# Strided attention: key sums as four extra columns of the output matmuls, and keys transposed in 32x32 blocks on VectorE

## The chip, the cores and the metric

The kernel runs on 1 core of one Trainium2 chip. The metric is the device time of one execution in microseconds (us). A profile covers the "span", from the first traced instruction of the core to the last. The time is longer than the span by about 2 us. The record marks a state, fast or slow, for every run. All runs of this study are marked fast, so they can be compared; each kernel is compared with runs of the kernel before from the same rounds.

Engines go by the profile's names: PE (TensorE, matmuls), PEld (PE's weight loads), DVE (VectorE), ACT (ScalarE), POOL (GpSimd) and SP (SyncE, which issues all loads and stores here). PSUM is the memory that the matmuls of this kernel write to, and a bank is one part of it. A "traced row" is any record of an engine in the trace, its waits included.

## The reference

```python
def setup_inputs():
    batch, heads, seq, dim = (8, 12, 1024, 64)      # Q, K, V float32, stride 64
def reference(Q, K, V, stride):
    scale = 1.0 / np.sqrt(dim)
    for i in range(seq):
        attend_positions = np.arange(0, seq, stride)         # 16 keys of 1024
        scores = np.einsum('bhqd,bhkd->bhqk', q, k) * scale
        weights = np.exp(scores - max);  weights /= sum + 1e-10
        result[:, :, i, :] = np.einsum('bhqk,bhkd->bhqd', weights, v)
```

All of Q is read and the whole output is written (25 MB each), while only 16 keys and values of each head take part.

## The kernel before

A group `g` is four heads, and there are 24 groups. One load brings 1 MB of Q, one store takes 1 MB of output. In between: a cast to bf16 (GpSimd), a transpose in 32x32 blocks (VectorE), scores (PE), exp (ScalarE), outputs (PE), and the normalization. The parts that the change touches, with cuts marked `...`:

```python
def key_rows(m):                      # keys: scaled copies, one for each head of a group
    kr = k_raw[:, 4 * m : 4 * m + 4].rearrange("p n (q f) -> p n f q", f=2)
    for h in range(4):
        nc.scalar.activation(out=k_m[:, 4 * m : 4 * m + 4, :, h], in_=kr,
                             func=AF.Copy, scale=slot_m[:, h : h + 1])
def keys(m):                          # ... turned by PE, copied out by ScalarE
    for u in range(2):
        kp = psum_sc.tile(...)
        for i in range(2):
            for f in range(2):
                nc.tensor.matmul(kp[:, i, :, f], lhsT=k_m[...], rhs=perm_k..., start=True, stop=True)
        nc.scalar.copy(k_t[...], kp[...])
def sums_mm(g):                       # sums over the keys: four matmuls
    sm = sm_ps[g] = psum_s.tile([P, 8, 32], FP32, name="sm", tag="sm")
    for q in range(4):
        nc.tensor.matmul(sm[32 * q : 32 * q + 32], lhsT=sel32,
                         rhs=wt[g][:, :, 32 * q : 32 * q + 32],
                         start=True, stop=True, tile_position=(0, 32 * q))
def sums_rec(g):                      # ... turned, then one reciprocal of 32 elements
    nc.vector.transpose(smt..., sm_ps[g]...)
    nc.vector.reciprocal(rec[g], smt[:, :, 0:4])
def outputs(g, c):                    # c = 0, 1: four token blocks in two PSUM banks
    ...
    for i in range(4):
        nc.tensor.matmul(ps[:, i]..., lhsT=wt[g][:, 4 * c + i], rhs=vb[g]..., start=True, stop=True)
def normalize(g, c):                  # 6 of 8 blocks on VectorE, 2 by ScalarE copy and GpSimd multiply
    ...
# loop over g, shortened: without the tests for the last groups
    transpose(g + 2); scores(g + 1); outputs(g, 0); outputs(g, 1); sums_mm(g + 1)
    values(g + 2); cast(g + 3); normalize(g, 0); normalize(g, 1); sums_rec(g + 1)
    ...; store(g); load(g + QBUFS)    # QBUFS = 9 loads are issued ahead
```

The softmax here doesn't subtract the row's maximum and nothing guards it: scores larger than these inputs give would overflow.

## Time and profile before

| | before |
|---|---|
| time, median of 6 runs | 129.81 us (129.78 to 130.21) |
| span of the profiled run | 127.6 us |
| bytes moved | 51.12 MB, 401 GB/s over the span |
| transfer queue's share of the 16 engines | 96.6% |
| busiest engine | VectorE (DVE), 74% |
| last compute ends, last packet ends | 114.8 us, 125.8 us |

The lines that carry this are in the prediction. Beside them, these are the groups of instructions that the change removes or alters (page of the kernel before; line, engine, operation, out<-in, shapes, count | busy us, mean ns | idle before, releaser):

```profile
L278 DVE TENSOR_TENSOR out_sb<-o_ps,rec 128x1024 f32<-128x1024 f32 (+1 forms) x48 | 43.0, 932 | 0.5 <-PE o_ps L264 0.3
L282 POOL TENSOR_TENSOR out_sb<-out_sb,rec 128x512 f32<-128x512 f32 x24 | 25.0, 1042 | 5.3 <-ACT out_sb L277 5.3
L242 PE MATMUL sm<-w,sel 128*32 128x256 bf16 x96 | 12.7, 298 | 8.0 <-ACT w L233 5.9
L255 DVE RECIPROCAL rec<-smt 128x32 f32<-128x32 f32 x24 | 8.5, 353 | 2.7 <-POOL vb L203 0.5
L251 DVE STREAM_TRANSPOSE smt<-sm 128x256 f32<-128x256 f32 x24 | 10.3, 427 | 0.0
q14 instruction: 4, 0.03, 0.1%
```

A reciprocal of 32 elements costs 353 ns, half of what a multiply of 512 costs (675 ns; the 932 is the mean of this and of 1188 ns for 1024 elements). The last line counts the packets of one queue that bring instructions within the span; the experiments come back to it.

### The profile page before, as it was taken

To read this page: it belongs to the slowest core of one execution; us is meant where nothing else is said; L and a number is where in the kernel's file an instruction comes from. 1 tells how busy PE (TensorE), PEld (TensorE's weight loads), DVE (VectorE), ACT (ScalarE), POOL (GpSimd) and SP (SyncE) were. 2 spreads that over 40 slices of the span, in tenths; PEclk is the share of its full clock that TensorE was granted. 3 is DMA by queue.
4 is the path that set the end of the run, shared out by engine and by line. 5 is a ranking of instruction groups with operands and counts; after the bars stand their busy time and mean duration, and the time that the engine had idled before them with its cause. 6 is when DMAs were issued, how large, how long until landed. Compare 5 with 4: busy or idle time off the path is not lost. (4 is left out here: it accounts for less than half of the span.)

```text
span 127.6 us, 1413 instructions
## 1 busy us (share of the span) xinstructions
PE 74.9 (59%) x412; PEld 35.9 (28%) x412; DVE 94.8 (74%) x136; ACT 58.8 (46%) x91; POOL 90.5 (71%) x93
## 2 busy tenths in 40 slices
PE   0008399857777787778877396396395495920000
PEld 0003044333443433333333153142142241510000
DVE  6935639999998999999999669669678687890000
ACT  0453443996379775666555353443442541610000
POOL 8983499999969999996865965955956959150000
PEclk9999999999999999999999859959958965798555
DMA  2999989899899999899899899998998999999980
GB/s 61 373 315 483 452 370 483 349 398 475 372 431 444 393 444 467 367 472 447 362 480 431 372 490 406 398 501 347 444 470 352 452 403 429 424 426 426 429 370 39
DMA packets 7911, 51.20 MB, mean 401 GB/s; under 512 B 3872, under 2 KB 3872, under 8 KB 3872
## 3 DMA queue, kind: packets, MB, share of 16 engines
q1 hardware_dynamic: 7904, 51.12, 96.6%
q8 instruction: 3, 0.05, 0.2%
q14 instruction: 4, 0.03, 0.1%
HBM read 25.95 MB, written 25.17 MB: 401 GB/s over the span
## 5 line engine op out<-in xcount | busy, mean ns | idle before, releaser
L211 POOL CAST qb<-qn 128x2048 bf16<-128x2048 f32 x24 | 45.3, 1890 | 16.2 <-DVE out_sb L278 9.7
L233 ACT ACTIVATE w<-sc 64x512 bf16<-64x512 f32 x48 | 35.3, 736 | 44.5 <-PE sc L222 43.9
L278 DVE TENSOR_TENSOR out_sb<-o_ps,rec 128x1024 f32<-128x1024 f32 (+1 forms) x48 | 43.0, 932 | 0.5 <-PE o_ps L264 0.3
L222 PE MATMUL sc<-qt,k_t 128*128 128x512 bf16 x96 | 30.6, 447 | 18.2 <-DVE qt L215 17.2
L215 DVE STREAM_TRANSPOSE qt<-qb 128x1024 int32<-128x1024 int32 x24 | 29.2, 1215 | 15.3 <-POOL qb L211 15.3
L264 PE MATMUL o_ps<-vb,w 128*128 128x256 bf16 x192 | 31.6, 306 | 1.1 <-DVE out_sb L278 0.4
L282 POOL TENSOR_TENSOR out_sb<-out_sb,rec 128x512 f32<-128x512 f32 x24 | 25.0, 1042 | 5.3 <-ACT out_sb L277 5.3
L264 PEld LDWEIGHTS <-w 128*128 128x128 bf16 x192 | 19.8, 109 | 17.7 <-DVE out_sb L278 9.4
L222 PEld LDWEIGHTS <-k_t 128*128 128x128 bf16 x96 | 9.4, 103 | 30.8 <-issue 22.7
L242 PE MATMUL sm<-w,sel 128*32 128x256 bf16 x96 | 12.7, 298 | 8.0 <-ACT w L233 5.9
L203 POOL TENSOR_TENSOR vb<-mask,v_rep 128x256 bf16<-128x256 bf16 x24 | 16.0, 668 | 1.8 <-DVE v_rep L196 1.8
L277 ACT COPY out_sb<-o_ps 128x512 f32<-128x512 f32 x24 | 14.0, 585 | 2.9 <-POOL out_sb L282 1.5
L255 DVE RECIPROCAL rec<-smt 128x32 f32<-128x32 f32 x24 | 8.5, 353 | 2.7 <-POOL vb L203 0.5
L251 DVE STREAM_TRANSPOSE smt<-sm 128x256 f32<-128x256 f32 x24 | 10.3, 427 | 0.0
L242 PEld LDWEIGHTS <-sel 128*32 128x32 bf16 x96 | 4.7, 94 | 17.8 <-issue 14.9
L175 PE MATMUL kp<-perm_k,k_m 128*128 128x128 bf16 x24 | 2.3, 250 | 9.3 <-ACT k_m L165 9.3
L165 ACT ACTIVATE k_m<-k_raw,slot_m 128x256 bf16<-128x256 f32 x12 | 5.3, 518 | 1.2 <-DVE slot_m L153 1.2
L175 PEld LDWEIGHTS <-k_m 128*128 128x128 bf16 x24 | 1.7, 112 | 9.5 <-ACT k_m L165 9.3
L136 POOL MEMSET k_t<- 128x4608 bf16 x1 | 3.9, 3937 | 0.0
L183 ACT CAST k_t<-kp 128x512 bf16<-128x512 f32 x6 | 3.2, 589 | 0.9 <-PE kp L175 0.7
L165 ACT ACT_TABLE_LOAD x1 | 1.3, 1283 | 5.0 <-DMA k_raw<-in_K_dram 5.0
L146 DVE TENSOR_SCALAR s_sel<-col,slot_f 128x4 bf16<-128x4 int16 x1 | 3.1, 3142 | 0.1
(22 smaller groups left out, 10.8 us busy)
## 6 DMA issues: line engine op xcount, KB each, us to landing
qn<-in_Q_dram SPq DMA_DIRECT2D x24, 1024.0 KB, 17.6
out_dram<-out_sb SPq DMA_DIRECT2D x24, 1024.0 KB, 17.3
k_raw<-in_K_dram SPq DMA_DIRECT2D x1, 384.0 KB, 4.2
v_raw<-in_V_dram SPq DMA_DIRECT2D x1, 384.0 KB, 7.2
```

Source lines behind the costliest of these rows:

```text
L203: nc.gpsimd.tensor_tensor(out=vb[g], in0=mask, in1=v_rep[:, g // 2, g % 2].unsqueeze(1).to_broadcast([P, 4, D]), op=ALU.mult,)
L211: nc.gpsimd.tensor_copy(out=qb[g], in_=qn[g])
L215: nc.vector.transpose(qt[g].bitcast(I32), qb[g].bitcast(I32))
L222: nc.tensor.matmul(sc, lhsT=k_t[:, g, f, NK * (1 - e) : NK * (1 - e) + P], rhs=_ap_with(q, [q.ap[0], [D, 8], [16 * D, 2], [2, 32]], extra_ ...
L233: nc.scalar.activation(out=_ap_with(wa, [wa.ap[0], [P, 8], [1, 2], [2, 32]], extra_offset=64 * a), in_=sc[64 * a : 64 * a + 64].rearrange( ...
L242: nc.tensor.matmul(sm[32 * q : 32 * q + 32], lhsT=sel32, rhs=wt[g][:, :, 32 * q : 32 * q + 32], start=True, stop=True, tile_position=(0, 3 ...
L251: nc.vector.transpose(smt.rearrange("p i r -> p (i r)"), sm.rearrange("p i r -> p (i r)"))
L255: nc.vector.reciprocal(rec[g], smt[:, :, 0:4])
L264: nc.tensor.matmul(ps[:, i].rearrange("p s d -> p (s d)"), lhsT=wt[g][:, 4 * c + i], rhs=vb[g].rearrange("p s d -> p (s d)"), start=True, ...
L277: nc.scalar.copy(part(i0 + n, 4 - n), ps[:, n:4])
L278: nc.vector.tensor_tensor(out=part(i0, n), in0=ps[:, 0:n], in1=fact(i0, n), op=ALU.mult)
L282: nc.gpsimd.tensor_tensor(out=part(i0 + n, 4 - n), in0=part(i0 + n, 4 - n), in1=fact(i0 + n, 4 - n), op=ALU.mult,)
```

## The change

The intent: PE, ScalarE and VectorE spend instructions on sums and keys that can be had as a by-product. The values' operand gets four more columns that select the head, so an output matmul writes the four sums beside its 256 columns, in a PSUM bank of its own, already in the layout that the normalization needs. The keys are turned by VectorE's block transpose and small copies, without PE. The diff, cut to its core:

```diff
-    psum_o = ctx.enter_context(tc.tile_pool(name="po", bufs=2, space=bass.MemoryType.PSUM))
-    psum_s = ctx.enter_context(tc.tile_pool(name="psm", bufs=2, space=bass.MemoryType.PSUM))
+    psum_o = ctx.enter_context(tc.tile_pool(name="po", bufs=3, space=bass.MemoryType.PSUM))
...
+    v_bufs = []
+    for i in range(3):
+        v = const.tile([P, 4 * D + 4], BF16, name=f"v{i}")
+        nc.vector.tensor_copy(out=v[:, 4 * D :], in_=s_sel)
+        v_bufs.append(v)
...
     def key_rows(m):
-        (four scaled copies on ScalarE)
+        nc.scalar.copy(k_bf[:, part], k_raw[:, part])
+        nc.vector.transpose(k_r[:, part]... as int32, k_bf[:, part]... as int32)
-    def keys(m):
-        (8 matmuls, 2 copies)
+    def keys(m, c):
+        for s in range(4):
+            op = nc.vector.tensor_copy if m == 0 and s >= 2 else nc.scalar.copy
+            op(k_t[dst : dst + 32, ...], k_r[src : src + 32, ...])
...
-    def sums_mm(g): ...
-    def sums_rec(g): ...
     def outputs(g, c):                       # now c = 0 .. 3, two token blocks each
-        for i in range(4):
+        ps = psum_o.tile([P, 2, 512], FP32, name="o_ps", tag="o")
+        for i in range(2):
             nc.tensor.matmul(
+                ps[:, i, 0 : 4 * D + 4], lhsT=wt[g][:, 2 * c + i], rhs=vb[g],
                 start=True, stop=True)
-    def normalize(g, c): ...
+        ...                                  # r, o, to, by: views of the tiles
+        nc.vector.reciprocal(r, ps[:, :, 4 * D : 4 * D + 4])
+        if c < 3:
+            nc.vector.tensor_tensor(out=to, in0=o, in1=by, op=ALU.mult)
+        else:
+            nc.scalar.copy(to, o)
+            nc.gpsimd.tensor_tensor(out=to, in0=to, in1=by, op=ALU.mult)
...
```

More of the change, by code (lines that the diff above doesn't have):

```diff
@@ L80 @@
     qt_pool = ctx.enter_context(tc.tile_pool(name="qt", bufs=2))
-    vb_pool = ctx.enter_context(tc.tile_pool(name="vb", bufs=3))
     rec_pool = ctx.enter_context(tc.tile_pool(name="rec", bufs=2))
     psum_sc = ctx.enter_context(tc.tile_pool(name="psc", bufs=2, space=bass.MemoryType.PSUM))
-    psum_o = ctx.enter_context(tc.tile_pool(name="po", bufs=2, space=bass.MemoryType.PSUM))
-    psum_s = ctx.enter_context(tc.tile_pool(name="psm", bufs=2, space=bass.MemoryType.PSUM))
+    psum_o = ctx.enter_context(tc.tile_pool(name="po", bufs=3, space=bass.MemoryType.PSUM))
     ctx.enter_context(tc.manual_schedule())
@@ L109 @@
     id_v = identity.rearrange("p (c b a k) -> p c b a k", c=2, b=2, a=2)
-    perm_k = const.tile([P, 2, 2, 2, NK], BF16, name="perm_k")
     perm_v = const.tile([P, 2, 2, 2, 2, NK], BF16, name="perm_v")
@@ L118 @@
     nc.gpsimd.iota(col4, pattern=[[1, 4]], base=0, channel_multiplier=0)
-    for c in range(2):
-        for a in range(2):
-            nc.gpsimd.tensor_copy(out=perm_k[:, c, a], in_=id_v[:, c, :, a])
     for c in range(2):
@@ L148 @@
     )
-    sel32 = const.tile([P, 32], BF16, name="sel32")
-    nc.vector.memset(sel32, 0.0)
-    nc.vector.tensor_copy(out=sel32[:, 0:4], in_=s_sel)
-    slot_m = const.tile([P, 4], FP32, name="slot_m")
-    nc.vector.tensor_copy(out=slot_m, in_=s_sel)
+    v_bufs = []
[3 more added lines that the diff above has]
+        v_bufs.append(v)
     mask = const.tile([P, 4, D], BF16, name="mask")
     nc.vector.tensor_copy(out=mask, in_=s_sel.unsqueeze(2).to_broadcast([P, 4, D]))
-    k_m = const.tile([P, NC, 2, 4, 32], BF16, name="k_m")
+    k_bf = const.tile([P, NC, D], BF16, name="k_bf")
+    k_r = const.tile([P, NC, D], BF16, name="k_r")
     v_bf = const.tile([P, NC, D], BF16, name="v_bf")
@@ L162, in key_rows @@
     def key_rows(m):
-        kr = k_raw[:, 4 * m : 4 * m + 4].rearrange("p n (q f) -> p n f q", f=2)
-        for h in range(4):
-            nc.scalar.activation(
-                out=k_m[:, 4 * m : 4 * m + 4, :, h], in_=kr,
-                func=AF.Copy, scale=slot_m[:, h : h + 1],
-            )
-    def keys(m):
-        for u in range(2):
-            kp = psum_sc.tile([P, 2, 2, 2, 4 * NK], FP32, name="kp", tag="sc")
-            for i in range(2):
-                for f in range(2):
-                    nc.tensor.matmul(
-                        kp[:, i, :, f],
-                        lhsT=k_m[:, 4 * m + 2 * u + i, f].rearrange("p h q -> p (h q)"),
-                        rhs=perm_k.rearrange("p c a b k -> p c (a b k)"),
-                        start=True, stop=True,
-                    )
-            g0 = 8 * m + 4 * u
-            dst = k_t[:, g0 : g0 + 4]
-            nc.scalar.copy(
-                _ap_with(dst, [dst.ap[0], [KW, 8], [32, 4], [1, NK]], extra_offset=NK),
-                kp.rearrange("p i c f (s k) -> p (i c f) s k", s=4),
+        part = slice(4 * m, 4 * m + 4)
+        nc.scalar.copy(k_bf[:, part], k_raw[:, part])
+        nc.vector.transpose(
+            k_r[:, part].rearrange("p n d -> p (n d)").bitcast(I32),
+            k_bf[:, part].rearrange("p n d -> p (n d)").bitcast(I32),
+        )
+    def keys(m, c):
+        for s in range(4):
+            src, dst, col = 32 * (2 * c + s % 2), 32 * (2 * (s % 2) + s // 2), NK + 32 * s
+            op = nc.vector.tensor_copy if m == 0 and s >= 2 else nc.scalar.copy
+            op(
+                k_t[dst : dst + 32, 8 * m + c : 8 * m + 8 : 2, :, col : col + NK],
+                k_r[src : src + 32, 4 * m : 4 * m + 4].rearrange(
+                    "p n (a k f) -> p a n f k", a=2, f=2
+                )[:, s // 2],
             )
@@ L190, in value_rows @@
         for c in range(2):
-            vp = psum_s.tile([P, NC // 2, D], FP32, name="vp", tag="sm")
+            vp = psum_sc.tile([P, NC // 2, D], FP32, name="vp", tag="sc")
             nc.tensor.matmul(
@@ L196, in value_rows @@
             nc.vector.tensor_copy(out=v_rep[:, 6 * n : 6 * n + 6, c], in_=vp)
-    qb, qt, wt, vb, rec, out_sb, o_ps, sm_ps = {}, {}, {}, {}, {}, {}, {}, {}
+    qb, qt, wt, vb, rec, out_sb = {}, {}, {}, {}, {}, {}
     def values(g):
-        vb[g] = vb_pool.tile([P, 4, D], BF16, name="vb", tag="vb")
+        vb[g] = v_bufs[g % 3]
         nc.gpsimd.tensor_tensor(
-            out=vb[g], in0=mask,
+            out=vb[g][:, 0 : 4 * D].rearrange("p (s d) -> p s d", s=4), in0=mask,
             in1=v_rep[:, g // 2, g % 2].unsqueeze(1).to_broadcast([P, 4, D]),
@@ L237, in scores @@
             )
-    def sums_mm(g):
-        sm = sm_ps[g] = psum_s.tile([P, 8, 32], FP32, name="sm", tag="sm")
-        for q in range(4):
-            nc.tensor.matmul(
-                sm[32 * q : 32 * q + 32], lhsT=sel32,
-                rhs=wt[g][:, :, 32 * q : 32 * q + 32],
-                start=True, stop=True, tile_position=(0, 32 * q),
-            )
-    def sums_rec(g):
-        sm = sm_ps[g]
-        smt = rec_pool.tile([P, 8, 32], FP32, name="smt", tag="smt")
-        nc.vector.transpose(
-            smt.rearrange("p i r -> p (i r)"), sm.rearrange("p i r -> p (i r)")
-        )
-        rec[g] = rec_pool.tile([P, 8, 4], FP32, name="rec", tag="rec")
-        nc.vector.reciprocal(rec[g], smt[:, :, 0:4])
     def outputs(g, c):
@@ L260, in outputs @@
             out_sb[g] = out_pool.tile([P, 4, 8, D], FP32, name="out_sb", tag="out_sb")
-        ps = psum_o.tile([P, 4, 4, D], FP32, name="o_ps", tag="o")
-        o_ps[g, c] = ps
-        for i in range(4):
+            rec[g] = rec_pool.tile([P, 8, 4], FP32, name="rec", tag="rec")
+        ps = psum_o.tile([P, 2, 512], FP32, name="o_ps", tag="o")
+        for i in range(2):
             nc.tensor.matmul(
-                ps[:, i].rearrange("p s d -> p (s d)"), lhsT=wt[g][:, 4 * c + i],
-                rhs=vb[g].rearrange("p s d -> p (s d)"),
+                ps[:, i, 0 : 4 * D + 4], lhsT=wt[g][:, 2 * c + i], rhs=vb[g],
                 start=True, stop=True,
             )
-    def normalize(g, c):
-        ps = o_ps[g, c]
-        i0 = 4 * c
-        n = 4 if c == 0 else 2
-        part = lambda k, m: out_sb[g][:, :, k : k + m].rearrange("p s i d -> p i s d")
-        fact = lambda k, m: rec[g][:, k : k + m].unsqueeze(3).to_broadcast([P, m, 4, D])
-        if n < 4:
-            nc.scalar.copy(part(i0 + n, 4 - n), ps[:, n:4])
-        nc.vector.tensor_tensor(
-            out=part(i0, n), in0=ps[:, 0:n], in1=fact(i0, n), op=ALU.mult
-        )
-        if n < 4:
-            nc.gpsimd.tensor_tensor(
-                out=part(i0 + n, 4 - n), in0=part(i0 + n, 4 - n),
-                in1=fact(i0 + n, 4 - n), op=ALU.mult,
-            )
+        r = rec[g][:, 2 * c : 2 * c + 2]
+        o = ps[:, :, 0 : 4 * D].rearrange("p i (s d) -> p i s d", s=4)
+        to = out_sb[g][:, :, 2 * c : 2 * c + 2].rearrange("p s i d -> p i s d")
+        by = r.unsqueeze(3).to_broadcast([P, 2, 4, D])
+        nc.vector.reciprocal(r, ps[:, :, 4 * D : 4 * D + 4])
[4 more added lines that the diff above has]
+            nc.gpsimd.tensor_tensor(out=to, in0=to, in1=by, op=ALU.mult)
     def store(g):
@@ L297 @@
     cast(1)
+    keys(0, 0)
     transpose(0)
-    keys(0)
+    scores(0)
+    keys(0, 1)
     nc.vector.tensor_copy(out=v_bf, in_=v_raw)
-    scores(0)
     transpose(1)
@@ L306 @@
     cast(2)
-    sums_mm(0)
-    sums_rec(0)
     for g in range(NG):
@@ L313 @@
             scores(g + 1)
-        outputs(g, 0)
-        outputs(g, 1)
-        if g + 1 < NG:
-            sums_mm(g + 1)
         if g + 2 < NG:
@@ L321 @@
             cast(g + 3)
-        normalize(g, 0)
-        normalize(g, 1)
-        if g + 1 < NG:
-            sums_rec(g + 1)
+        for c in range(4):
+            outputs(g, c)
         if g in (1, 5):
             key_rows(g // 4 + 1)
-        if g in (2, 6):
-            keys(g // 4 + 1)
-        if g == 3:
+        if g in (2, 3, 6, 7):
+            keys(g // 4 + 1, g % 4 - 2)
+        if g == 4:
             value_rows(1)
```

## The prediction

> **What bounds the kernel now.** I read the busy table and the slices first, then the transfer rows, then SyncE's timeline, then VectorE's, and last the stretches of the tail.
>
> ```profile
> PE 74.9 (59%) x412; PEld 35.9 (28%) x412; DVE 94.8 (74%) x136; ACT 58.8 (46%) x91; POOL 90.5 (71%) x93
> DMA  2999989899899999899899899998998999999980
> q1 hardware_dynamic: 7904, 51.12, 96.6%
> ```
>
> No engine is above 74%, while the transfer engines are at 8 or 9 tenths in every slice but the first and the last, and the one transfer queue fills 96.6% of their time. The program must move 51.12 MB. I counted the packet records of the trace: from 9 us on, between 15.2 and 16.3 of the 16 engines carry a packet in every microsecond until 123.7 us, so there is no hole a change of compute could close.
>
> ```profile
> 105.00:110.00 5.00, 3.43 (x16) 1.50 (x15) 3.66 (x5) 1.36 (x4) 3.55 (x4) 0.50 1.02 429
> 110.00:115.00 5.00, 2.24 (x16) 1.11 (x14) 4.45 (x6) 1.88 (x3) 2.08 (x2) 0.99 1.01 423
> 115.00:120.00 5.00, 0.00 (x0) 0.00 (x0) 0.00 (x0) 0.00 (x0) 0.00 (x0) 0.69 1.02 428
> 120.00:125.00 5.00, 0.00 (x0) 0.00 (x0) 0.00 (x0) 0.00 (x0) 0.00 (x0) 0.50 0.85 357
> ```
>
> These are stretches (columns: PE, PEld, DVE, ACT, POOL busy, granted clock, transfer share, GB/s). All compute ends before 115 us; transfers go on at 423 to 428 GB/s for 9 us more. That is a backlog of stores already issued. The chain that ended last is therefore a queue of bytes, and the compute before it has about 9 us to spare less one transfer.
>
> ```profile
> 67.30 0.59 SPq L35 DMA_DIRECT2D out_dram<-out_sb  x1
> 69.64 0.47 SPq L35 DMA_DIRECT2D qn<-in_Q_dram  x1
> 72.19 0.59 SPq L35 DMA_DIRECT2D out_dram<-out_sb  x1
> ```
>
> On SyncE, one store follows the other after 4.89 us here. A group of four heads is one load and one store of 1.05 MB, and 2.10 MB at 428 GB/s is 4.90 us: the loop runs at transfer speed. What the engines could do is seen where neither loads nor buffers hold them up:
>
> ```profile
> 44.99 0.35 DVE L255 RECIPROCAL rec<-smt 128x32 f32<-128x32 f32 x1
> 45.26 1.19 DVE L215 STREAM_TRANSPOSE qt<-qb 128x1024 int32<-128x1024 int32 x1
> 46.37 1.78 DVE L278 TENSOR_TENSOR out_sb<-o_ps,rec 128x1024 f32<-128x1024 f32 x2
> 48.07 0.42 DVE L251 STREAM_TRANSPOSE smt<-sm 128x256 f32<-128x256 f32 x1
> 48.60 0.35 DVE L255 RECIPROCAL rec<-smt 128x32 f32<-128x32 f32 x1
> ```
>
> VectorE goes round in 48.60 - 44.99 = 3.61 us without a gap. So it has 4.90 - 3.61 = 1.29 us of slack per group, and this slack is what the change spends.
>
> **What the Trainium skill says.** "DMA: Bandwidth & Descriptors", section "Where 436 GB/s comes from", puts the fabric's ceiling at 435 GB/s, and says that about 358 GB/s of HBM per core binds a transfer between HBM and SBUF. The trace agrees with the first (423 to 434 GB/s held for tens of microseconds) and not with the second; the measurement decides: this kernel runs at the ceiling. "VectorE: DVE Perf Modes", section "First, the fixed hardware budget", says that a reciprocal is an iterative divide with a repeat count of 8. The trace fits a dear reciprocal: 32 elements take 353 ns, while an f32 multiply of 512 takes 675. "Perfetto Trace Analysis", section "Optimizing Scalar/DVE Operations", warns of a cost per instruction, larger from PSUM, part of which overlaps the next instruction. The trace shows the overlap: a multiply that starts at 39.85 and lasts 0.67 is followed at 40.45 us, a step of 0.60.
>
> **The change part by part**, per group unless said.
>
> *PE.* Removed: four key-sum matmuls with their weight loads (96 of 298 ns and of 94 ns, 17.4 us busy in all). Added: four columns on each of eight output matmuls, 256 to 260, at some 306 x 4/256 = 5 ns each, nothing. At the start and twice later, 24 key matmuls go. PE is not the bound: 0 us.
>
> *VectorE.* Removed: the transpose of the sums (427 ns) and one reciprocal of 32 elements. The normalizing multiplies were one of 1024 and one of 512 elements, and become three of 512. Added: four reciprocals of 8 elements out of PSUM. Their duration: transposes of 1024 and 256 elements take 1215 and 427 ns, so 1.03 ns an element and 164 ns fixed. With the same fixed part the reciprocal costs (353 - 164)/32 = 5.9 ns an element, and one of 8 costs 164 + 47 = 0.21 us (an estimate; the most it could be is 0.35, all fixed). Each multiply must wait for its own reciprocal, and such a dependent pair shows a gap of 0.11 us (48.07 + 0.42 to 48.60). So the steps are: transpose of the queries 1.11 (45.26 to 46.37); three times 0.21 + 0.10 + 0.60 = 0.91, so 2.73; the fourth reciprocal 0.21 less the overlap of 0.08, so 0.13. Sum 3.97 us against 3.61: 0.36 us longer, still under 4.90.
>
> *GpSimd.* Unchanged: 1890 + 1042 + 668 ns = 3.60 us. But its multiply now waits for the fourth reciprocal, the last thing that VectorE does for a group. From there multiply, values and cast take 3.6 us before the transpose that needs them, one whole round (3.97) later. It fits, by 0.3 us.
>
> *ScalarE.* The same copy of 512 elements; key rows and key copies only at the start and in six iterations.
>
> *PSUM.* Three output buffers of two banks for four blocks a group. The fourth block waits until the first is read; it then has two blocks of VectorE work (1.8 us) to get two matmuls (0.6 us) and the copy (585 ns) done. No wait on VectorE.
>
> *Start.* Keys are ready earlier without four scaled copies, eight matmuls and two copies out, but the scores start at 10.91 us because the first transpose ends at 10.77, behind the cast that waited for its load until 7.60. This stays. The second load is what the next cast waits for (11.76). So the keys gain nothing. The first store comes later: VectorE's first multiply begins at 19.79 now; then 2.73 + 0.21 puts the last reciprocal at 22.7, GpSimd's 1.04 makes 23.8, and the store is issued at about 23.9 instead of 22.09. In the packet records the initial loads last until 28.0 us, and from issue to the first packet the key load shows 1.1 us (0.73 to 1.83). So 23.9 is 3 us early enough: no hole.
>
> *End.* The 24th store is issued at the latest at 23.9 + 23 x 3.97 = 115.2, plus about 2 us for what is done once (two value copies of 524 ns, two small key transposes, and perhaps 0.4 us where the value matmuls now borrow the score buffers): 117. It was 114.9. The transfers end at 123.8 if never starved; the last store needs 2.45 us of them and 1.1 us ahead of them, so any issue before 120.2 costs nothing. 3 us remain. On the path to the end, the sum is 0.
>
> **The rivals.**
> 1. *VectorE becomes the bound.* For: the slack counted to the end is thin; each 0.01 us on a reciprocal is 0.04 a group and 0.9 us at the end, so 0.25 instead of 0.21 eats the 3 us. A PSUM source and two separated runs of four might be dearer than my fixed part. Against: multiplies from PSUM show the same fixed part (675 and 1188 ns for 512 and 1024: 162 ns). At 0.28 the last store would be at 123.4 and the time 133; at 0.35, 24 rounds of 4.53 give about 139.
> 2. *A chain of hand-overs becomes the bound*: multiply on GpSimd behind the fourth reciprocal, then the cast, then the transpose; or PE, which can now run less far ahead. With 0.3 us of margin in the first a round of 4.2 to 4.3 is possible: the last store at 122 to 124, time 131.5 to 134.
> 3. *The start gets faster and all follows.* For: PE and ScalarE are relieved there. Against: the transfers are busy from 3 us on with loads that wait for no compute; earlier keys can't start a byte earlier. At most 0.3 us.
> 4. *The transfer pattern shifts.* Stores are later against loads, so the small dips (15.2 to 15.6 engines at 34, 61 and 97 us) move. Worth 0.1 to 0.3 us either way.
>
> **Range and chances.** The base is 129.81 unchanged, plus 0.1 for rivals 1 and 2 weighed: 129.9. Below, nothing but rival 4: 129.4. Above, a VectorE round of about 4.15 us instead of 3.97 (last store 121.2) gives 131 and a little more: 131.6. Faster by 2% would need 2.6 us of fewer bytes or fuller engines: 0.01. Slower by 2% needs a round of about 4.25 us or more: 0.09. The rest is 0.90.
>
> **What would show it.** Right: the queue's share stays near 96.6%, the transfers end near 124 us of the span, the unhindered VectorE round is 3.9 to 4.1 us, four reciprocals of about 0.2 us, first store near 24 us, last store issued before 120. Wrong: a transfer share that sinks in the last 30 us, VectorE without idle time to the end, or reciprocals over 0.25 us. GpSimd waiting for VectorE's reciprocals and transposes waiting for the cast in turn would show rival 2.

## The result, and the profile after

| | before | after |
|---|---|---|
| time, median of 6 runs | 129.81 us | 129.36 us (129.15 to 129.72) |
| ratio, 95% interval | | 0.9959, 0.9941 to 0.9977 |
| span of the profiled run | 127.6 us | 127.9 us |
| time less span, same run | 2.14 us | 1.79 us |
| first store issued | 22.1 us | 24.6 us |
| last store issued | 114.9 us | 118.3 us |
| last packet ends | 125.8 us | 126.2 us |

A ratio is the mean time of one kernel's fast runs over that of the other's of the same rounds, so it is not quite the ratio of the medians quoted beside it.

The change is within 2%, as predicted, but 0.04 us below the range, whose lower end was 129.4. And the profile has no gain to show: this profiled run's span is 0.3 us longer than that of the kernel before. The page of the kernel after, in the parts shown before:

```profile
PE 65.9 (52%) x292; PEld 28.2 (22%) x292; DVE 100.3 (78%) x215; ACT 55.9 (44%) x96; POOL 90.2 (71%) x89
DMA  2999989999899899999899899899999999999970
q1 hardware_dynamic: 7904, 51.12, 96.4%
q14 instruction: 5, 0.04, 0.1%
L244 DVE TENSOR_TENSOR out_sb<-o_ps,rec 128x512 f32<-128x512 f32 x72 | 49.8, 692 | 2.5
L247 POOL TENSOR_TENSOR out_sb<-out_sb,rec 128x512 f32<-128x512 f32 x24 | 25.0, 1042 | 22.0 <-ACT out_sb L246 22.0
L246 ACT COPY out_sb<-o_ps 128x512 f32<-128x512 f32 x24 | 14.1, 586 | 45.3 <-DVE rec L242 16.8
L242 DVE RECIPROCAL rec<-o_ps 128x8 f32<-128x8 f32 x96 | 18.3, 192 | 0.8 <-PE o_ps L234 0.8
```

PE lost 9 us of work and VectorE gained 5.5. The transfers' row is as full as before (96.4 against 96.6%). The reciprocals of 8 elements take 192 ns (estimate: 210). GpSimd's wait for ScalarE's copy has grown from 5.3 to 22.0 us, and the copy now waits for the reciprocal. The stretches of the tail (PE, PEld, DVE, ACT, POOL busy, clock, transfer share, GB/s):

```profile
105.00:110.00 5.00, 2.92 (x16) 1.40 (x17) 4.86 (x11) 1.97 (x4) 3.89 (x4) 1.00 1.02 428
110.00:115.00 5.00, 3.24 (x19) 1.29 (x17) 4.80 (x15) 2.53 (x4) 1.58 (x2) 0.98 1.01 424
115.00:120.00 5.00, 0.23 (x2) 0.00 (x0) 1.42 (x4) 0.59 (x1) 1.55 (x2) 0.50 1.01 424
120.00:125.00 5.00, 0.00 (x0) 0.00 (x0) 0.00 (x0) 0.00 (x0) 0.00 (x0) 0.50 0.82 346
```

Compute now runs into the stretch from 115 us on, where it had ended before, yet the transfers flow at the same 424 to 428 GB/s. SyncE's timeline shows that the loop is no longer paced by transfers (after; start us, us, instruction):

```profile
76.65 0.59 SPq L35 DMA_DIRECT2D out_dram<-out_sb  x1
...
80.37 0.59 SPq L35 DMA_DIRECT2D out_dram<-out_sb  x1
...
84.78 0.59 SPq L35 DMA_DIRECT2D out_dram<-out_sb  x1
...
88.51 30.29 SPq L35 DMA_DIRECT2D out_dram<-out_sb  x9
```

Stores follow each other by 3.72 and 4.41 us in turn, 4.07 on average, where they had been 4.9 apart. That is not a speed-up: before, compute ran ahead until it had to wait for loads; now it is slower and never catches up with them, and the backlog of transfers is what hides this. The last line is nine stores merged: the last was issued at 88.51 + 30.29 less its own 0.5, so at 118.3 us. What sets these rounds, the timeline of all engines shows (after, from 54 us; the bracket is the idle time before and its releaser):

```profile
54.00 0.20 DVE L242 RECIPROCAL rec<-o_ps 128x8 f32<-128x8 f32 x1
54.23 0.59 ACT L246 COPY out_sb<-o_ps 128x512 f32<-128x512 f32 x1 [0.49 <-DVE rec L242]
...
54.71 1.25 DVE L203 STREAM_TRANSPOSE qt<-qb 128x1024 int32<-128x1024 int32 x1 [0.51 <-POOL qb L199]
...
54.90 1.04 POOL L247 TENSOR_TENSOR out_sb<-out_sb,rec 128x512 f32<-128x512 f32 x1 [0.22 <-ACT out_sb L246]
...
55.90 0.67 POOL L191 TENSOR_TENSOR v<-mask,v_rep 128x256 bf16<-128x256 bf16 x1
...
56.51 1.89 POOL L199 CAST qb<-qn 128x2048 bf16<-128x2048 f32 x1
...
58.37 0.20 DVE L242 RECIPROCAL rec<-o_ps 128x8 f32<-128x8 f32 x1
58.48 1.19 DVE L203 STREAM_TRANSPOSE qt<-qb 128x1024 int32<-128x1024 int32 x1
```

The copy of the fourth block does not need the reciprocal's result, yet it starts 0.03 us after the reciprocal ends (0.03 to 0.08 us in all 24 groups). Both read the same PSUM tile. The Trainium skill, "PSUM — Partial Sum Buffer", section "PSUM bank collisions raise a hardware error", says that two engines must not touch the same bank at once, reads against reads included, so such reads have to be put in order. The trace agrees in so far as the copy never overlaps the reciprocal; no run here shows a collision. So reciprocal, copy, multiply, values, cast and the next transpose are one chain of 4.28 us from 54.20 to 58.48, longer than VectorE's own round of 3.72. The rounds alternate because the chain makes VectorE wait only every second time: when it waits the 0.51 us before 54.71, its fourth reciprocal is already done (54.00), so the next chain gets a head start and its transpose comes 3.77 us after this one; in the round after that VectorE waits again (4.36 us).

So there are two questions. Where do 0.45 us come from, when nothing in the span got faster? And is the slower round really free?

### The profile page after: what moved, and what is told of

It reads as the page before. It is cut to its first block, busy times and chain, and to the rows that moved or that the text cites. A ratio compares the mean times of both kernels' runs of the same rounds, so it can differ in the third digit from the quotient of the medians.

```text
span 127.9 us, 1221 instructions
## 1 busy us (share of the span) xinstructions
PE 65.9 (52%) x292; PEld 28.2 (22%) x292; DVE 100.3 (78%) x215; ACT 55.9 (44%) x96; POOL 90.2 (71%) x89
## 3 DMA queue, kind: packets, MB, share of 16 engines
q1 hardware_dynamic: 7904, 51.12, 96.4%
## 4 chain that ended last, share of the span: by engine, by line
POOL 46%; issue 25%; DMA 16%; SPq 1%; DVE 1%; POOLq 1%; ACT 0%
POOL qb L199 27%; POOL v L191 10%; DMA out_dram<-out_sb 9%; POOL out_sb L247 9%; DMA qn<-in_Q_dram 7%; DVE qt L203 1%; POOLq L318 1%; SPq L35 1%; ACT out_sb L246 0%; SPq L100 0%; DVE v_rep L184 0%; SPq L98 0%; POOLq L199 0%; POOLq L247 0%; POOLq L191 0%
## 5 line engine op out<-in xcount | busy, mean ns | idle before, releaser
L234 PE MATMUL o_ps<-v,w 128*128 128x260 bf16 x192 | 40.6, 314 | 34.9 <-DVE out_sb L244 28.0
L244 DVE TENSOR_TENSOR out_sb<-o_ps,rec 128x512 f32<-128x512 f32 x72 | 49.8, 692 | 2.5
L234 PEld LDWEIGHTS <-w 128*128 128x128 bf16 x192 | 17.4, 108 | 61.4 <-DVE out_sb L244 40.7
L242 DVE RECIPROCAL rec<-o_ps 128x8 f32<-128x8 f32 x96 | 18.3, 192 | 0.8 <-PE o_ps L234 0.8
L191 POOL TENSOR_TENSOR v<-mask,v_rep 128x256 bf16<-128x256 bf16 x24 | 16.0, 668 | 2.3 <-DVE v_rep L184 2.3
L210 PEld LDWEIGHTS <-k_t 128*128 128x128 bf16 x96 | 10.4, 108 | 24.6 <-issue 16.6
L169 ACT COPY k_t<-k_r 32x128 bf16<-32x128 bf16 x20 | 5.9, 295 | 2.4 <-DVE k_r L159 2.1
L180 PE MATMUL vp<-v_bf,perm_v 128*128 128x384 bf16 x4 | 1.6, 412 | 2.7 <-DVE v_rep L184 2.4
L169 DVE COPY k_t<-k_r 32x128 bf16<-32x128 bf16 x4 | 2.5, 628 | 0.1
L184 DVE CAST v_rep<-vp 128x384 bf16<-128x384 f32 x4 | 2.0, 532 | 0.6 <-PE vp L180 0.6
L158 ACT CAST k_bf<-k_raw 128x256 bf16<-128x256 f32 x3 | 1.2, 405 | 2.9 <-DMA k_raw<-in_K_dram 2.8
```

The costliest lines, as they stand in the source:

```text
L169: op(k_t[dst : dst + 32, 8 * m + c : 8 * m + 8 : 2, :, col : col + NK], k_r[src : src + 32, 4 * m : 4 * m + 4].rearrange("p n (a k f) -> p ...
L191: nc.gpsimd.tensor_tensor(out=vb[g][:, 0 : 4 * D].rearrange("p (s d) -> p s d", s=4), in0=mask, in1=v_rep[:, g // 2, g % 2].unsqueeze(1).t ...
L210: nc.tensor.matmul(sc, lhsT=k_t[:, g, f, NK * (1 - e) : NK * (1 - e) + P], rhs=_ap_with(q, [q.ap[0], [D, 8], [16 * D, 2], [2, 32]], extra_ ...
L234: nc.tensor.matmul(ps[:, i, 0 : 4 * D + 4], lhsT=wt[g][:, 2 * c + i], rhs=vb[g], start=True, stop=True,)
L242: nc.vector.reciprocal(r, ps[:, :, 4 * D : 4 * D + 4])
L244: nc.vector.tensor_tensor(out=to, in0=o, in1=by, op=ALU.mult)
```

## The experiments

Eleven runs were made, all of the changed kernel or the one before, unchanged (e1, e11) or with a small edit, and all correct except one. The summary; "outside" is time less span, from each run's own pair (spans to 0.1 us, so a single value is good to 0.05; the six runs of the kernel before in the first comparison have no spans and count in the medians alone):

| kernel | runs | median us | ratio (95%) | mean span | outside, mean (range) |
|---|---|---|---|---|---|
| before, as the comparison | 33 | 129.80 to 129.95 by batch | 1 | 127.75 | 2.15 (2.09 to 2.21) |
| after, first comparison | 6 | 129.36 | 0.9959 (0.9941 to 0.9977) | 127.58 | 1.79 (1.75 to 1.82) |
| e1 before again | 5 | 129.84 | 1.0001 (0.9988 to 1.0014) | 127.74 | 2.15 (2.11 to 2.21) |
| e2 keys only | 5 | 129.58 | 0.9973 (0.9961 to 0.9985) | 127.78 | 1.78 (1.74 to 1.82) |
| e3 sums only | 6 | 129.54 | 0.9971 (0.9958 to 0.9985) | 127.73 | 1.80 (1.77 to 1.83) |
| e4 after, PE padded | 5 | 129.51 | 0.9972 (0.9960 to 0.9984) | 127.76 | 1.79 (1.76 to 1.82) |
| e5 before, VectorE + 8 | 4 | 129.41 | 0.9958 (0.9943 to 0.9972) | 127.65 | 1.77 (1.73 to 1.80) |
| e6 before, GpSimd + 8 | 4 | 129.93 | 1.0001 (0.9988 to 1.0014) | 127.78 | 2.15 (2.12 to 2.18) |
| e7 after, split block first | 6 | 129.69 | 0.9982 (0.9966 to 0.9998) | 127.88 | 1.79 (1.73 to 1.83) |
| e8 after, VectorE delayed | 4 | 133.31 | 1.0247 (1.0221 to 1.0274) | 131.43 | 1.80 (1.74 to 1.82) |
| e9 transfers alone | 4 | 127.96 | 0.9843 (0.9815 to 0.9870) | 126.17 | 1.80 (1.75 to 1.83) |
| e10 before, VectorE + 2 | 6 | 129.73 | 0.9990 (0.9974 to 1.0005) | 127.80 | 1.93 (1.90 to 1.95) |
| e11 after again | 6 | 129.47 | 0.9968 (0.9943 to 0.9993) | 127.72 | 1.80 (1.77 to 1.84) |

### e1: the kernel before again

The edit: none.

> The kernel before, unchanged, to learn its span in several runs (only one is known: 127.6 us of a time of 129.77, so 2.14 us lie outside the traced span; the changed kernel has 1.75 to 1.82 us outside in six runs and spans of 127.4 to 127.9). Theory A, the gain of 0.45 us lies outside the span: time less span stays near 2.1 us in all its runs, spans 127.5 to 127.9, about those of the changed kernel. Theory B, the transfers inside the span are packed better by the change: its spans are about 0.4 us longer than those of the changed kernel and time less span is about 1.8 in most runs. Ratio to the kernel before: 1.000 for both.

Measured: 2.11 to 2.21 us outside in these five runs and in the eleven of the comparison, with spans of 127.6 to 128.0. Theory A, a gain outside the span, holds; theory B, better packed transfers, finds no support.

### e2: only the keys

```diff
 (the kernel before, with the change's key_rows, keys and their calls)
-    perm_k, slot_m, k_m and the 24 key matmuls
+    k_bf, k_r: nc.scalar.copy, nc.vector.transpose, small copies
```

> Only the keys' half of the change: keys by 32x32 blocks on VectorE, the sums as before. Theory A (outside the span, by the length of the programs): PE loses only 24 of its 412 matmuls, so most of the gap of 0.35 us outside stays: 129.7 to 129.8. Theory C, that ready keys start the work earlier: the gain of 0.45 is here, 129.3 to 129.4. Theory B (stores come later against loads because VectorE's round is longer): 129.8, as the round stays at 3.6 us.

Measured: 129.58, ratio 0.9973. This fits none of the three: more gain than theory A allowed if PE's length were the cause, less than theory C promised. What does hold is the place: 1.78 us outside, and spans (127.6 to 127.9) like those of the kernel before.

### e3: only the sums

```diff
 (the changed kernel, with perm_k, slot_m, k_m, key_rows and keys of the kernel before)
-    k_bf, k_r and the copies
+    the 24 key matmuls and their copies
```

> Only the sums' half: four extra columns, the keys by PE as before. Theory A: PE loses 96 matmuls with their weight loads, so most of the gain shows, outside the span: 129.4 to 129.5, time less span 1.8. Theory B: the gain shows too, 129.4, but in the span. Theory C: 129.8.

Measured: 129.54, ratio 0.9971, 1.80 outside. Each half alone brings the full 0.36 us outside the span, and both together bring no more. So it is a step and not a sum of savings. Removed work that adds up would not do that.

### e4: PE's count restored

```diff
         for i in range(2):
+            for _ in range(PAD[2 * c + i]):          # (1, 0, 1, 0, 1, 1, 1, 0)
+                nc.tensor.matmul(ps[:, i, 4 * D : 4 * D + 4], lhsT=wt[g][:, 2 * c + i],
+                                 rhs=vb[g][:, 4 * D : 4 * D + 4], start=True, stop=True)
             nc.tensor.matmul(ps[:, i, 0 : 4 * D + 4], ...)
```

> The changed kernel with 120 added matmuls of four columns that write what the real ones overwrite, so that PE has as many matmuls and weight loads as before (412). [...] Theory A, if it is PE's instruction count that sets the time outside: back to 129.75 to 129.85 with 2.1 us outside. Theory B and C: stays at 129.4 with 1.8 us outside.

Measured: 129.51 with 1.79 outside. (The added matmuls took 182 ns each, 21.3 us in all, and the mean span, 127.76, did not grow.) PE's count is not the cause, and theory A in the form I had given it fell. The trace's packet records gave the next form. Apart from the loads and stores they hold a few packets of 8 KB on one instruction queue (q14), and their last one differs:

| profiled run | last instruction packet, us from the span's start | span ends | time |
|---|---|---|---|
| before | 129.23 to 129.73 | 127.63 | 129.77 |
| e1, before again | 129.23 to 129.68 | 127.62 | 129.77 |
| after | 127.89 to 128.20 | 127.93 | 129.72 |
| e2 | 127.30 to 127.66 | 127.59 | 129.37 |
| e3 | 127.75 to 128.10 | 128.00 | 129.78 |
| e4 | 127.47 to 127.94 | 127.69 | 129.47 |

(If the time is counted from the span's start, the two columns compare directly.) All have a packet close to the span's end, but only the kernel before has one more, 1.6 us behind it, and its time ends within 0.1 us of that packet. Whose program is it? In e2 a packet came at 116.7 us, when VectorE had run 192 of its 195 traced rows. The kernel before has 189, so the same place in the program would lie just behind its end. The traces of the changed kernel and its variants (after, e3, e4, and later e7, e8 and e11), with 235 to 265 rows, have such a packet too, far from the end, at 96.2 to 104.1 us, and there VectorE has run 193 to 197 rows each time.

### e5 and e6: eight more instructions on VectorE, or on GpSimd

```diff
     nc.gpsimd.memset(k_t[:, 8:NG], 0.0)
+    spare = const.tile([P, 8], FP32, name="spare")
+    for i in range(8):
+        nc.vector.memset(spare[:, i : i + 1], 0.0)      # e6: nc.gpsimd.memset
```

> The kernel before with eight one-element memsets added on VectorE at the start, where it idles. All 17 runs of the kernel before had 2.11 to 2.21 us outside the span and all 27 runs of the four other kernels 1.74 to 1.83, with the same spans; so the gain lies outside. Padding PE back to its old count did not bring it back, so it is not PE's count. The traces show one 8 KB packet of instructions at 129.23 us, 1.6 us behind the end of the span, only in the kernel before. Theory A2: it belongs to VectorE, whose program is 189 traced rows long in the kernel before, while in the keys-only kernel (195 rows) such a packet comes at row 192, inside the span. Eight more instructions pull it into the span: time less span 1.8, time 129.4 to 129.6, ratio about 0.997. Theory A3 (another engine's program, or the epilogue for another reason): 2.15 us outside, 129.85.

> The control: the same eight memsets on GpSimd instead. Theory A2 (VectorE's program): nothing changes, 2.15 us outside and 129.85. Theory A3 with GpSimd as the engine: 1.8 outside, 129.5.

(The first text counts 27 runs of the four other kernels; it should be 22.) Measured: e5 129.41, ratio 0.9958, 1.77 outside; e6 129.93, ratio 1.0001, 2.15 outside. Eight useless instructions on VectorE make the kernel before as fast as the changed one, and the same eight on GpSimd do nothing. The pages show the packet move: this is the instruction queue's row, first of e5, then of e6.

```profile
q14 instruction: 5, 0.04, 0.1%
```

```profile
q14 instruction: 4, 0.03, 0.1%
```

Five packets within the span, as in the kernel after, against four, as in the kernel before. In e5 the additional one came at 117.0 us, while VectorE sat at row 194 of 197 and waited for the stores. In e6 it came at 129.40, ending at 129.95 with the time at 129.94.

### e10: two more instructions

The edit, against e5:

```diff
-    for i in range(8):
+    for i in range(2):
         nc.vector.memset(spare[:, i : i + 1], 0.0)
```

> The kernel before with two instead of eight memsets added on VectorE. Eight pulled the packet of instructions into the span (at row 194 of 197) and took 0.37 us off the time outside. With two the program is 191 traced rows long, so a boundary near row 194 still lies behind the end. If it is the place of that boundary, nothing is gained: 2.15 us outside and 129.9. If any change of VectorE's program or of the layout does it: 1.8 and 129.5.

Measured: 129.73, 1.93 us outside (1.90 to 1.95 in six runs). Neither: the packet still lies behind the span, as I had expected, but it starts at 128.67 instead of 129.23 and ends 0.3 us before the time does. So there is no all or nothing, and my sentence that nothing is gained while the packet lies behind the end was wrong. A reading that fits: the nearer the boundary lies to the end of the program, the earlier the packet is asked for, and the less of it is in the way. But here the time goes on for 0.3 us after the packet, so the time outside is not simply set by the packet's end.

### e11: the changed kernel again

The edit: none.

> The changed kernel again, on another chip and in other rounds. Its first six runs had spans of 127.4 to 127.9 us, 0.1 to 0.2 below the mean of the kernel before, beside 0.36 us less outside the span. If the part in the span is scatter, the ratio here is 0.9965 to 0.998 (0.36 us of 129.9 is 0.9972) and the spans have the mean of the kernel before, 127.7 to 127.8; if the changed kernel's transfers really are better packed, the ratio is again 0.996 or less and the spans average 127.6 or less.

Measured: ratio 0.9968, mean span 127.72, 1.80 outside. So the 0.53 us of the first ratio (0.9959) were 0.36 outside and 0.17 in the span, and the second part did not repeat. Over both batches the changed kernel's twelve spans average 127.65 against 127.75 in 33 of the kernel before, less than their own scatter (127.4 to 128.3) lets one call a difference.

### e7: the split block first

```diff
-        if c < 3:
+        if c > 0:
             nc.vector.tensor_tensor(out=to, in0=o, in1=by, op=ALU.mult)
         else:
             nc.scalar.copy(to, o)
```

> The changed kernel, but with block 0 of a group instead of block 3 going over ScalarE's copy and GpSimd's multiply. In the changed kernel the copy starts only after the fourth reciprocal (20 to 30 ns after it ends), so copy, multiply, values, cast and the next transpose form one chain, and VectorE's rounds alternate between 3.72 and 4.41 us. If that chain is what makes the mean round 4.07 instead of 3.72, the rounds are 3.72 here wherever the loads don't hold, and the last store is issued at 112 to 116 instead of 118.3 us. If transfers bound the end (my prediction), the time stays all the same at 129.2 to 129.6 with 1.8 us outside. If the hand-over chain did reach the end, the time falls by 1 us or more.

Measured: 129.69, spans 127.5 to 128.3, 1.79 outside. The chain is indeed gone. VectorE's transposes and SyncE's last stores (e7, timelines):

```profile
47.26 1.24 DVE L203 STREAM_TRANSPOSE qt<-qb 128x1024 int32<-128x1024 int32 x1
...
50.98 1.23 DVE L203 STREAM_TRANSPOSE qt<-qb 128x1024 int32<-128x1024 int32 x1
...
54.70 1.24 DVE L203 STREAM_TRANSPOSE qt<-qb 128x1024 int32<-128x1024 int32 x1
```

```profile
71.84 0.59 SPq L35 DMA_DIRECT2D out_dram<-out_sb  x1
...
76.96 0.59 SPq L35 DMA_DIRECT2D out_dram<-out_sb  x1
...
81.86 0.59 SPq L35 DMA_DIRECT2D out_dram<-out_sb  x1
```

VectorE's rounds are 3.72 us from 47 us on. The stores follow each other by some 4.9 us from 67 us on, and VectorE's rounds from 81 us on, as in the kernel before. The last store is issued at 116.6 us instead of 118.3, a little later than the 112 to 116 that I had expected. The time does not follow (129.69 against 129.36 and 129.47 of the changed kernel, in other batches; it is 0.09 above the range that I gave for no effect, but the intervals of the ratios overlap): a chain of 0.35 us a round that I had overlooked costs nothing at the end.

### e8: VectorE delayed

```diff
         for c in range(4):
             outputs(g, c)
+        nc.vector.memset(spare, 0.0)          # 576 elements, 0.54 us
```

> The changed kernel with one more VectorE memset of about 0.6 us per group. The last store was issued at 118.3 us, and by my prediction an issue up to 120.2 costs nothing. If the round grows by 0.25 to 0.6 us, the last store is issued at 124 to 132 us, and the time is 129.4 plus (issue - 120.2), so 133 to 141 us. If the end had more slack than I worked out, the time grows by clearly less than issue - 120.2; if transfers were not the bound at all, by the whole shift of the issue from 118.3.

Measured: 133.31 (ratio 1.0247). VectorE's rounds are 4.32 us, and the last store was issued at 126.1 us in the profiled run, which took 133.52. By my formula it should have been 129.4 + 126.1 - 120.2 = 135.3; had transfers not been the bound, the shift of the issue from 118.3 would have made 137.2. So a transfer-bound end with more slack than I had worked out. The stretches (e8) show what it looks like when the backlog is used up:

```profile
100.00:110.00 10.00, 6.34 (x32) 2.82 (x30) 9.62 (x20) 5.30 (x9) 7.64 (x7) 0.92 0.97 409
110.00:115.00 5.00, 3.15 (x12) 1.44 (x12) 4.79 (x12) 2.63 (x4) 4.18 (x5) 0.67 0.87 365
115.00:120.00 5.00, 3.80 (x14) 1.71 (x14) 4.28 (x11) 2.06 (x4) 1.39 (x2) 0.64 0.55 224
120.00:125.00 5.00, 1.86 (x8) 0.57 (x8) 4.63 (x13) 1.17 (x2) 1.04 (x1) 0.70 0.70 288
```

The rate falls to 224 GB/s while VectorE is still busy. The last packet ends at 129.99, 3.9 us after the issue. In the two traces of the changed kernel the last packet ends at 126.2 and 126.3. So an issue up to about 126.2 - 3.9 = 122.3 us is free (an estimate from these traces), not 120.2, and the changed kernel has 4 us left of what were 7.4.

### e9: the transfers alone

```diff
+    still = const.tile([P, 32 * D], FP32, name="still")
+    nc.vector.memset(still, 0.0)
+    for g in range(NG):
+        _copy(nc, (out of group g), still)          # wrong on purpose
+        if g + QBUFS < NG:
+            load(g + QBUFS)
+    return
```

> The kernel before with its loads and stores alone, wrong on purpose: the same 51.1 MB in the same order and sizes, stores of a constant tile, no compute to wait for. If transfers bound the end in both kernels, the last packet lands near 126 us of the span here too (125.8 before, 126.2 after), and with some 1.8 us outside the time is 129.0 to 129.6. If the compute still costs something in either kernel, this is shorter by it: 128.5 or less.

Measured: 127.96 (127.53 to 128.45). My 129.0 to 129.6 was missed: the kernel that computes pays 1.6 us of span for it (127.73 in the same rounds against 126.17). One pair of traces splits the 1.0 us between them: the last packet ends at 125.30 instead of 125.83, and from there to the span's end it is 1.36 us instead of 1.80. The page of e9 has the queue fuller than either kernel's:

```profile
q1 hardware_dynamic: 7904, 51.12, 97.1%
```

Against the changed kernel's 129.47 (another batch) the transfers alone, in this order, make 98.8% of the time, so no rearrangement of the compute can be worth more than about 1.2%. A part can be read from the packet records: the small dips that the prediction saw at 34, 61 and 97 us are where a 16 KB instruction packet takes one of the 16 engines for about 1.05 us (34.08 to 35.16, 61.33 to 62.37, 96.69 to 97.73), and e9 has neither such packets in its span nor dips. These three and the three of 8 KB (0.31 us each) that come while transfers run are 4.1 us of one engine, so an estimated 0.26 us of all 16. What the rest of the 1.6 us consists of stays open.

## Why the prediction was wrong

The verdict "within 2%" and its mechanism, an end that transfers bound, were right; the number 129.9 was 0.5 us too high and the range missed by 0.04 us. Point by point:

**The base.** This is the step that failed: "The base is 129.81 unchanged" and, for the lower end, "Below, nothing but rival 4: 129.4". I carried over the whole time, span and rest, and asked only what changes in the span. Of the 129.81 us, 2.15 lie outside the span, and the change made that 1.79: a term of -0.36 us that my sum did not have. (It takes 129.81 to 129.45, the edge of the range; on which side of the edge a batch falls is scatter in the span. The repeat e11, with 129.47, lies inside.) What the runs show of its cause: the time outside depends on the length of VectorE's program, and most likely on where a boundary between two packets of its instructions falls. Eight instructions added on VectorE (e5) switch it, eight on GpSimd (e6) and 120 matmuls on PE (e4) do not, two on VectorE (e10) bring 0.22 of the 0.36 us. The packet of instructions moves with it in every trace. That the end of the kernel waits for this packet is inferred and not shown: the time ends within 0.1 us of the packet in three traces where it came behind the span (before, e1, e6), but 0.3 us after it in the fourth (e10). No run takes the packet away by itself, and none makes the changed kernel's program longer until a boundary falls behind its end again.

**The transfers bound the end.** Right, and tested. VectorE's work grew by 5.5 us, the last store went out 3.4 us later, and the span did not move beyond its scatter (e11). Making the compute faster brings nothing (e7), delaying the last store to 126.1 us brings 4 us (e8). "So there is no hole a change of compute could close" was a little too strong: without compute 1.6 us of span go (e9).

**VectorE's steps.** The reciprocal was 192 ns for an estimate of 210. The gap between a reciprocal and the multiply that needs it was 0.03 us in all 72 pairs (as from 53.16 + 0.20 to 53.39), not 0.11, so VectorE's own round is 3.72 us and not 3.97.

**GpSimd's hand-over.** "It fits, by 0.3 us" was wrong. I had left out that ScalarE's copy must follow the fourth reciprocal, which adds 0.59 us and a hand-over to the chain. The chain, rival 2, sets the mean round to 4.07. That the two errors nearly cancel is luck: 4.07 for 3.97, first store at 24.6 for 23.9, last at 118.3 for 117.

**The slack at the end.** "Any issue before 120.2 costs nothing" was 2 us on the safe side (e8: 122.3). I had counted from 123.8 us, where the engines stop being all busy, and not from the last packet near 126. With the smaller slack I gave the slower side 0.09; it deserved less.

**Rival 4.** The dips whose moving was to be worth 0.1 to 0.3 us are not idle time but instruction packets (see e9).

**Keys and start.** Right: with the change's keys alone (e2) the first store is issued at 21.9 instead of 22.1 us, and spans are unchanged.

## What to carry to other kernels

Where transfers are full to the end, as here, work moved between engines is free until the last store is issued too late, and the quantity to watch is that issue time against the last packet, not busy shares. When two kernels differ by a few tenths of a microsecond, subtract each run's span first: here, what differed outside it had nothing to do with the amount of work saved, and could be had by eight useless instructions on one engine. Halves that each bring the whole gain were the sign of such a step.

## What the Trainium skill lacked or had wrong

- "Runtime: NRT & Kernel Launch", section "Instruction fetch mechanics", says that crossing a boundary between blocks of instructions is mostly hidden, and that blocks are of 16 KiB. In the span the trace agrees: VectorE's rounds in the changed kernel stay 3.77 and 4.36 us across the packet at 99.32 us. At the end of a program, if the reading above is right, it is not hidden: 0.36 us (2.15 against 1.79 us outside the span), 0.14 us with two more instructions. The packets of the queue that carried the one concerned are of 8 KB; packets of 16 KB appear on another queue only (3 in the kernel before with 412 matmuls, 2 in the kernel after with 292).
- No page says that adding instructions may make a kernel faster, as by moving the place of such a boundary: e5, 129.41 against 129.95 us.
- "DMA: Bandwidth & Descriptors", section "Where 436 GB/s comes from", has about 358 GB/s of HBM per core as what binds a transfer between HBM and SBUF. For this kernel on one core the sentence does not hold: the core held 424 to 428 GB/s until its last stores, near the 435 that the section gives for the fabric. Elsewhere the skill does limit the figure to two cores that share their memory, so it is this sentence that needs the condition.
- No page has the price of a reciprocal: 353 ns for 32 elements from SBUF, 192 for 8 from PSUM.
